# Four small loads moved to GpSimd's queue at the start, and two table copies moved behind the last key product

## The chip, the core and the metric

The kernel runs on one core of one Trainium2 chip. The metric is the device time in microseconds (us) of one launch, the median of several runs. The engines are named as in the profile: PE (TensorE matmul), PEld (its weight loads), DVE (VectorE), ACT (ScalarE), POOL (GpSimd), SP (SyncE, which only starts transfers). ACTq, SPq and POOLq are the issuing sides of these engines. Each engine runs its instructions strictly in the order in which they stand in its queue; an instruction that waits holds everything behind it.

## What is computed

Two transformer blocks on a sequence of 256 tokens of width 1024, all in fp32. The part that matters here is the beginning of the first block and three small inputs of the second:

```python
# first block
h    = rms_norm(x, norm_mix_pre)
proj = h @ w_in                              # q, k_c, v_c, k_s, v_s, k_w, v_w, gates, u, v
kc   = compress_tokens(k_c, cmp_pos_k, ...)  # 2-layer MLP over blocks of 32 keys
lg   = q @ k.T + rel_bias[bucket(distance)]  # three attention branches, softmax, gates
# second block
mod  = silu(c) @ ada_w + ada_b               # c: the conditioning vector, 1024 numbers
rel  = positions[key] - positions[query]     # 256 integers, bucketed
bias = rel_bias_2[bucket(rel)]               # table of 32 x 16
```

## The kernel before

Every large product takes its weights through `wload` (line 270, a transfer on SP's queue into one of six `raw` tiles) and `wsplit` (line 292): ACT writes the high part `hi` (line 301), DVE the low part `lo` (line 302), and PE adds three products per tile in `mm3` (lines 309 to 311). A `raw` tile is free for the next transfer when its `lo` has been written.

The first stage computes, in this order: the key and value projection (`kv`, 512 columns; its evaluation `ev_kv` makes `kd` tiles on DVE at line 788, which PE transposes at line 795), the bias table of the first block (`bias_tables`), the q projection (512 columns, `ev_q`, whose result DVE copies at line 784), `conditioning` (silu of the conditioning vector, in tile `c8`), `pos_prep` (positions split into parts by six DVE operations for the 256-wide tile `pr` and six for the 2-wide tile `pc`, the table `rel_bias_2` in tile `tb` split into three bf16 parts, and the clipped distances `relc`), the beginning of `compress` for the keys (tile `X`, line 846), and the last key product: the window projection of 280 columns (`ev_w`). Then a weave of attention, compression, conditioning rows (`adas_pe`) and the u and v projections follows, until about 150 us.

`bias_tables` stores an 8 x 384 row to DRAM (line 912), loads it back as the table `B1` of 1 MB spread over the partitions (line 914, ACT's queue), and at lines 916 and 917 DVE copies two strided pieces of `B1` into `Bc`, which the first attention logits need.

The order of instructions in each queue is made when the program is built: a scheduler places them by priority and by its own estimate of times, inside `queued(...)` blocks that keep instructions of ACT, DVE and SP behind marked ones. So a moved line of code can move instructions of other lines on the same engine. ACT's queue issues the transfers of `c8`, of the constants `tri` (128 x 818 numbers), of `pr`, `pc` and of the four 32-row pieces of `tb`. POOL sets constants, makes the identity matrix (masks.py), issues the transfers of `mod_quarters` (line 541), and computes the powers at line 226.

Of the kernel before, what the change touches and what calls it, by code (L numbers as in the profile page):

```python
# [20 lines left out]
P = 128  # L21
S = 256
# [66 lines left out]
def body(tc, I, O):  # L89
    nc = tc.nc  # L90
    v, s, g, pe, sy = nc.vector, nc.scalar, nc.gpsimd, nc.tensor, nc.sync
# [3 lines left out]
    def nm(x):  # L95
        cnt[0] += 1
        return f"{x}_{cnt[0]}"

    def pool(name, bufs=1, space=None, side=None):
        kw = {"reuse_waits": "tile"}  # L100
        if space is not None:
            kw["space"] = space
            if space is DRAM:
                kw = {"space": space}
        if side:
            kw["side"] = side
        return tc.tile_pool(name=name, bufs=bufs, **kw)
# [7 lines left out]
    def T(pl, shape, dt=F32, tag=None, bufs=1):  # L115
        n = nm(tag or "t")
        return pl.tile(list(shape), dt, name=n, tag=tag or n, bufs=bufs)
# [16 lines left out]
    def atb():  # L134
        return T(ps, [P, 512], tag="at", bufs=2)

    def scr(n=1024):
        return T(per, [P, 1024], tag="scr", bufs=NSCR)[:, :n]
# [4 lines left out]
    def run(gen):  # L143
        for _ in gen:
            pass
# [63 lines left out]
    tri = T(cst, [P, 2 * S + 2 * P + 50])  # L209
    cum = tri[:, 0:2 * S].rearrange("p (a l) -> p a l", a=2)  # L210
    o = 2 * S
# [58 lines left out]
    def wload(src3, shape, extra=(), tag="raw", bufs=None, pl=None):  # L270
        raw = T(pl or wp, [P, CH], tag=tag, bufs=bufs or NRAW)[:, :int(np.prod(shape))]
        raw = raw.rearrange("p (a n) -> p a n", a=shape[0])
        if src3 is not None:
            sy.dma_start(raw, src3)
        for d0, d1, src in extra:
            sy.dma_start(raw[:, :, d0:d1], src)
        return raw
# [27 lines left out]
    def ktile(W, k0, kn, c0, n):  # L305
        return W[k0 * P:(k0 + kn) * P, c0:c0 + n].rearrange("(a p) n -> p a n", p=P)

    def mm3(out, xh, xl, wh, wl, start, stop):
        pe.matmul(out, xh, wh, start=start, stop=False)  # L309
        pe.matmul(out, xh, wl, start=False, stop=False)  # L310
        pe.matmul(out, xl, wh, start=False, stop=stop)  # L311

    def groups(n, sizes):
        out, i = [], 0
        while i < n:
            k = sizes[min(len(out), len(sizes) - 1)]
            out.append(list(range(i, min(n, i + k))))
            i += k
        return out

    def proj(W, c0, n, KT, xT, evac, extra=None, sizes=(2,), bank=ma, pre=None):

        pc = max(1, CH // n)
        while KT % pc:
            pc -= 1
        xh, xl = xT
        accs = [bank()[:, :n], bank()[:, :n]]
        nch = KT // pc
        for grp in groups(nch, sizes):
            ws = {}  # L330
            for ci in grp:
                if pre and ci in pre:
                    raw = pre[ci]
                elif extra is None:
                    raw = wload(ktile(W, ci * pc, pc, c0, n), (pc, n))
                else:
                    raw = wload(None, (pc, n), [(d0, d0 + m, ktile(W, ci * pc, pc, cc, m)) for d0, cc, m in extra])
                ws[ci] = wsplit(raw, (pc, n))
            for t in range(2):
                sl = slice(t * P, (t + 1) * P)  # L340
                for ci in grp:
                    hi, lo = ws[ci]
                    for k in range(pc):
                        kk = ci * pc + k
                        mm3(accs[t], xh[:, kk, sl], xl[:, kk, sl], hi[:, k], lo[:, k], kk == 0, kk == KT - 1)
                if grp[-1] == nch - 1:
                    evac(t, accs[t])
                yield
# [167 lines left out]
    c8 = T(cst, [P, 8])  # L516
# [7 lines left out]
    T(cst, [P, 24])  # L524

    def conditioning():
        s.dma_start(tri, I["c_tri"])
        s.dma_start(c8, I["c_2"].rearrange("o (a p) -> p (o a)", p=P))
        s.activation(th8, c8, AF.Tanh, scale=0.5)
        v.scalar_tensor_tensor(th8, th8, 1.0, c8, op0=OP.add, op1=OP.mult)  # L530
        v.tensor_scalar(c8, th8, 0.5, None, op0=OP.mult)

    mods = T(dr, [6, D])

    gains = {1: "pre_norm_mix_2", 2: "post_norm_mix_2", 4: "pre_norm_ffn_2", 5: "post_norm_ffn_2"}
# [141 lines left out]
    pos = I["positions_2"]  # L677

    def pos_parts(dst_hi, dst_lo, dst_md, src):
        n = src.shape[-1]  # L680
        ti = T(pp, [P, S], I32, tag="pi", bufs=2)[:, :n]
        v.tensor_single_scalar(ti, src, 12, op=OP.arith_shift_right)
        v.tensor_copy(dst_hi, ti)
        ti = T(pp, [P, S], I32, tag="pi", bufs=2)[:, :n]
        v.tensor_single_scalar(ti, src, 4095, op=OP.bitwise_and)
        v.tensor_copy(dst_lo, ti)
        t2 = T(pp, [P, S], I32, tag="pi", bufs=2)[:, :n]
        v.tensor_single_scalar(t2, ti, 6, op=OP.arith_shift_right)
        v.tensor_copy(dst_md, t2)

    pmat = T(per, [P, 3, S])
    pcol = T(per, [P, 3, 2])
    rel_dr = T(dr, [S, S], BF)

    def pos_prep():
        pr = T(pp, [P, S], I32, tag="pi", bufs=2)
        s.dma_start(pr, bass.AP(tensor=pos.tensor, offset=pos.offset, ap=[[0, P], [1, S]]))
        pos_parts(pmat[:, 0], pmat[:, 1], pmat[:, 2], pr)
        pc = T(pp, [P, 2], I32)
        s.dma_start(pc, pos.rearrange("o (a p) -> p (o a)", p=P))  # L700
        pos_parts(pcol[:, 0], pcol[:, 1], pcol[:, 2], pc)

        tb = T(pp, [P, 4, 16])
        g.memset(tb, 0.0)
        for i in range(4):
            s.dma_start(tb[i * 32:(i + 1) * 32, i, :], I["rel_bias_2"])
        tbf = tb.rearrange("p a h -> p (a h)")
        v.tensor_scalar(tp[:, 0], tbf, -1.0, None, op0=OP.mult)
        rem = T(pp, [P, 64])
        v.scalar_tensor_tensor(rem, tbf, -1.0, tp[:, 0], op0=OP.mult, op1=OP.subtract)  # L710
        v.tensor_copy(tp[:, 1], rem)
        v.tensor_tensor(tp[:, 2], rem, tp[:, 1], op=OP.subtract)
        relc = scr(256).bitcast(BF).rearrange("p (k q) -> p k q", k=2)
        for k in range(2):
            ab = scr(512)
            a, b_ = ab[:, :S], ab[:, S:]
            v.tensor_scalar(a, pmat[:, 0], pcol[:, 0, k:k + 1], -4096.0, op0=OP.subtract, op1=OP.mult)
            v.tensor_scalar(b_, pmat[:, 1], pcol[:, 1, k:k + 1], -1.0, op0=OP.subtract, op1=OP.mult)
            v.tensor_tensor(a, a, b_, op=OP.add)
            v.tensor_scalar(relc[:, k], a, 120.0, -120.0, op0=OP.min, op1=OP.max)  # L720
        s.dma_start(rel_dr[:, :].rearrange("(k p) q -> p k q", p=P), relc)

    bias_dr = T(dr, [2, P, 16, S])

    def key_bias():
# [21 lines left out]
        for n in range(8):  # L747
# [7 lines left out]
            for t in range(2):  # L755
# [8 lines left out]
                    s.dma_start(bias_dr[t, :, :, k * P:(k + 1) * P], dst[t])  # L764
                yield

    with pool("a1") as ap:
        awg = pool("a1w")
        aw = awg.__enter__()
# [128 lines left out]
        B1 = T(ap, [P, 8, S])  # L898
        Bc = T(ap, [P, 2, 8, 16])

        def bias_tables():
            hf = scr()
            hot, fx = hf[:33, :384], hf[:8, 384:768]
            s.dma_start(hot, I["c_hot"])
            tab = T(aw, [33, 8], tag="tab")
            v.memset(tab[32:33, :], 1.0)
            s.dma_start(tab[0:32, :], I["rel_bias"])
            b = atb()
            pe.matmul(b[:8, :384], tab, hot, start=True, stop=True)
            v.tensor_copy(fx, b[:8, :384])  # L910
            scratch = T(dr, [8, 384])
            s.dma_start(scratch, fx)
            sc = scratch[:, :]
            s.dma_start(B1, bass.AP(tensor=sc.tensor, offset=sc.offset, ap=[[1, P], [384, 8], [1, S]]))
            g.memset(Bc, BIG)
            v.tensor_copy(Bc[:, 0, :, 0:7], B1[:, :, 96::-16])
            v.tensor_copy(Bc[:, 1, :, 0:15], B1[:, :, 224::-16])

        def attention():
            PTc = T(aw, [P, S], tag="PTc", bufs=1)  # L920
# [143 lines left out]
        with queued():  # L1064
            next(kv)
            run(kv)
            bias_tables()
            run(proj(W, 0, 512, 8, xT, ev_q))
            marks = mark()
            conditioning()  # L1070
            pos_prep()
            ck = compress(0, I["cmp_pos_k"][0], I["cmp_w1_k"][0], I["cmp_w2_k"][0])
            cv = compress(1, I["cmp_pos_v"][0], I["cmp_w1_v"][0], I["cmp_w2_v"][0])
            next(ck)
            ahead(3)
            run(proj(W, 1024, 280, 8, xT, ev_w))
        wa, wf = SCHED["a1"]
        with queued(marks=marks):
            weave((seq(ck, cv, mix(attention(), adas_pe((1, 0), aw, cws, ahead))), wa * 1.7),
# [159 lines left out]
    ap = latg.__enter__()  # L1239
# [143 lines left out]
    ap = atg.__enter__()  # L1383
# [205 lines left out]
```

## Time and profile before

| | us |
|---|---|
| median of 3 runs | 969.82 (967.96 to 969.91) |
| the profiled execution, its own time | 972.12 |
| its span, first to last instruction | 970.3 |
| PE busy | 921.8 (95% of the span) |
| DVE busy | 717.2 (74%) |
| ACT busy | 507.5 (52%) |
| POOL busy | 38.6 (4%) |
| granted PE clock, mean | 0.984 of full speed |

The profiled execution is 2.3 us longer than the median, and 1.8 us of it lie outside the span. The kernel is bound by PE nearly everywhere; what a change of small operations is worth has to be read from the few places where PE waits.

### The profile page before, as it was taken

Reading aid. Unit: us, or ns where it says so; the run is one execution under the profiler, and the core shown is the slowest. Engines: PE = TensorE matmul, PEld = TensorE weight load, DVE = VectorE, ACT = ScalarE, POOL = GpSimd, SP = SyncE. Lnnn points to the kernel's source line nnn. Section 1 sums busy time; section 2 is a strip of 40 time slices with the busy share of each in tenths; the row PEclk is TensorE's granted clock in tenths of the full one; section 3 lists DMA queues with packets and bytes.
Section 4 is the critical chain, followed back from the end, with each engine's and each line's share of the span. In section 5 each row is a group of like instructions: output and inputs, shape, how many; then the busy total and the mean of one; then the engine's idle time right before and its main releaser. Section 6 shows DMA issues by size and latency. Waiting matters only on the chain.

```text
span 970.3 us, 16176 instructions
## 1 busy us (share of the span) xinstructions
PE 921.8 (95%) x6161; PEld 778.1 (80%) x6161; DVE 717.2 (74%) x1305; ACT 507.5 (52%) x873; POOL 38.6 (4%) x63
## 2 busy tenths in 40 slices
PE   7899999979997999999799999999999999999997
PEld 6666667869996877897688679988977879999885
DVE  5767849487884559579988877889988885776544
ACT  5436536434542446466457548856763653444432
POOL 1000001000000002100000000000001010000000
PEclk9999999999999999999999999999999999999999
DMA  9887538678886596465444579687778667776651
GB/s 289 256 292 227 192 111 278 199 217 263 222 243 193 178 319 173 130 188 157 136 135 152 167 230 257 178 188 184 205 209 302 225 204 250 246 224 202 206 174 43
DMA packets 157113, 200.00 MB, mean 206 GB/s; under 512 B 14867, under 2 KB 118316, under 8 KB 157036
## 3 DMA queue, kind: packets, MB, share of 16 engines
q1 hardware_dynamic: 137840, 184.61, 63.4%
q10 hardware_dynamic: 16268, 8.30, 3.1%
q0 software_dynamic: 2928, 6.07, 2.1%
q8 instruction: 48, 0.79, 0.3%
q14 instruction: 29, 0.24, 0.1%
HBM read 193.39 MB, written 5.54 MB: 205 GB/s over the span
## 4 chain that ended last, share of the span: by engine, by line
PE 73%; DVE 9%; DMA 8%; issue 4%; ACT 3%; POOL 1%; SPq 0%; ACTq 0%; DVEq 0%; POOLq 0%
PE ma L311 6%; PE ma L309 6%; PE ma L310 6%; PE ma L388 6%; PE ma L390 6%; PE ma L389 5%; PE mb L388 5%; PE mb L389 5%; PE mb L390 5%; PE mb L310 4%; PE mb L309 4%; PE mb L311 4%; DMA t<-kb 3%; DVE lo L302 2%; DMA araw<-in_ada_w_dram 2%
## 5 line engine op out<-in xcount | busy, mean ns | idle before, releaser
L302 DVE TENSOR_TENSOR lo<-raw,hi 128x1024 fp32r<-128x1024 f32 (+2 forms) x242 | 291.7, 1212 | 117.1 <-ACT hi L301 113.3
L301 ACT CAST hi<-raw 128x1024 fp32r<-128x1024 f32 (+2 forms) x242 | 250.8, 1043 | 222.6 <-PE mb L311 75.8
L390 PE MATMUL ma<-xTh,lo 128*128 128x256 f32 x512 | 144.5, 282 | 6.8 <-DVE lo L302 6.7
L388 PE MATMUL ma<-xTh,hi 128*128 128x256 f32 x512 | 145.5, 284 | 1.6 <-ACT hi L301 1.6
L389 PE MATMUL ma<-xTl,hi 128*128 128x256 f32 x512 | 143.6, 280 | 0.0
L388 PE MATMUL mb<-xTh,hi 128*128 128x256 f32 x384 | 107.1, 279 | 0.0
L390 PE MATMUL mb<-xTh,lo 128*128 128x256 f32 x384 | 106.5, 277 | 0.0
L389 PE MATMUL mb<-xTl,hi 128*128 128x256 f32 x384 | 106.4, 277 | 0.0
L390 PEld LDWEIGHTS ma<-xTh,lo 128*128 128x128 f32 x512 | 97.5, 191 | 8.7 <-DVE lo L302 7.6
L388 PEld LDWEIGHTS ma<-xTh,hi 128*128 128x128 f32 x512 | 97.5, 190 | 4.7 <-ACT hi L301 2.0
L389 PEld LDWEIGHTS ma<-xTl,hi 128*128 128x128 f32 x512 | 97.6, 191 | 1.1 <-issue 0.8
L310 PE MATMUL ma<-lo,xTh 128*128 128x512 f32 (+2 forms) x192 | 74.8, 391 | 1.9 <-DVE lo L302 1.9
L309 PE MATMUL ma<-hi,xTh 128*128 128x512 f32 (+2 forms) x192 | 75.4, 395 | 0.0
L311 PE MATMUL ma<-hi,xTl 128*128 128x512 f32 (+2 forms) x192 | 75.1, 392 | 0.0
L388 PEld LDWEIGHTS mb<-xTh,hi 128*128 128x128 f32 x384 | 72.2, 188 | 1.2 <-issue 1.2
L390 PEld LDWEIGHTS mb<-xTh,lo 128*128 128x128 f32 x384 | 72.2, 188 | 0.4 <-DVE cva L1209 0.4
L389 PEld LDWEIGHTS mb<-xTl,hi 128*128 128x128 f32 x384 | 72.1, 188 | 0.2 <-issue 0.2
L310 PEld LDWEIGHTS ma<-lo,xTh 128*128 128x128 f32 x192 | 36.4, 189 | 10.2 <-DVE lo L302 2.9
L311 PEld LDWEIGHTS ma<-hi,xTl 128*128 128x128 f32 x192 | 36.4, 190 | 9.1 <-issue 2.4
L309 PEld LDWEIGHTS ma<-hi,xTh 128*128 128x128 f32 x192 | 36.6, 191 | 8.6 <-issue 1.9
L309 PE MATMUL mb<-hi,hTh 128*128 128x512 f32 x80 | 32.2, 402 | 0.0
L310 PE MATMUL ma<-lo,hTh 128*128 128x512 f32 x80 | 31.4, 392 | 0.5 <-DVE lo L302 0.5
(474 smaller groups left out, 1877.5 us busy)
## 6 DMA issues: line engine op xcount, KB each, us to landing
raw<-in_w_in_dram SPq DMA_DIRECT2D x80, 512.0 KB, 5.8
raw<-in_w_gate_up_dram SPq DMA_DIRECT2D x44, 512.0 KB, 7.7
raw<-in_w_ffn_in_dram SPq DMA_DIRECT2D x44, 512.0 KB, 4.8
raw<-in_w_down_dram SPq DMA_DIRECT2D x22, 512.0 KB, 4.6
raw<-in_w_ffn_out_dram SPq DMA_DIRECT2D x22, 512.0 KB, 4.5
cw<-in_ada_w_dram SPq DMA_DIRECT2D x16, 512.0 KB, 4.1
raw<-in_w_out_dram SPq DMA_DIRECT2D x16, 512.0 KB, 5.8
araw<-in_ada_w_dram SPq DMA_DIRECT2D x16, 512.0 KB, 11.7
```

Of the source, the lines that this page charges most:

```text
L301: s.copy(hi, raw)
L302: v.tensor_tensor(lo, raw, hi.bitcast(F32), op=OP.subtract)
L309: pe.matmul(out, xh, wh, start=start, stop=False)
L310: pe.matmul(out, xh, wl, start=False, stop=False)
L311: pe.matmul(out, xl, wh, start=False, stop=stop)
L388: pe.matmul(out, hi[:, k % pc, fs], xh[:, k], start=k == 0, stop=False)
L389: pe.matmul(out, hi[:, k % pc, fs], xl[:, k], start=False, stop=False)
L390: pe.matmul(out, lo[:, k % pc, fs], xh[:, k], start=False, stop=k == KT - 1)
```

## The change

`conditioning` no longer issues its two transfers. They, the two loads of the positions and the four of the table go out on POOL's queue (`g.dma_start` for `s.dma_start`). `pos_prep` becomes a generator in two pieces: the loads stand ahead of the first stage, the arithmetic where the whole stood before. The two copies into `Bc` move from `bias_tables` to a place behind the window projection.

```diff
     def conditioning():
-        s.dma_start(tri, I["c_tri"])
-        s.dma_start(c8, I["c_2"].rearrange("o (a p) -> p (o a)", p=P))
         s.activation(th8, c8, AF.Tanh, scale=0.5)
...
+    g.dma_start(c8, I["c_2"].rearrange("o (a p) -> p (o a)", p=P))
+    g.dma_start(tri, I["c_tri"])
     mods = T(dr, [6, D])
...
     def pos_prep():
         pr = T(pp, [P, S], I32, tag="pi", bufs=2)
-        s.dma_start(pr, bass.AP(tensor=pos.tensor, offset=pos.offset, ap=[[0, P], [1, S]]))
-        pos_parts(pmat[:, 0], pmat[:, 1], pmat[:, 2], pr)
+        g.dma_start(pr, bass.AP(tensor=pos.tensor, offset=pos.offset, ap=[[0, P], [1, S]]))
         pc = T(pp, [P, 2], I32)
-        s.dma_start(pc, pos.rearrange("o (a p) -> p (o a)", p=P))
-        pos_parts(pcol[:, 0], pcol[:, 1], pcol[:, 2], pc)
+        g.dma_start(pc, pos.rearrange("o (a p) -> p (o a)", p=P))
         tb = T(pp, [P, 4, 16])
         g.memset(tb, 0.0)
         for i in range(4):
-            s.dma_start(tb[i * 32:(i + 1) * 32, i, :], I["rel_bias_2"])
+            g.dma_start(tb[i * 32:(i + 1) * 32, i, :], I["rel_bias_2"])
+        yield
+        pos_parts(pmat[:, 0], pmat[:, 1], pmat[:, 2], pr)
+        pos_parts(pcol[:, 0], pcol[:, 1], pcol[:, 2], pc)
...
+        yield
...
+    pos_terms = pos_prep()
+    next(pos_terms)
     with pool("a1") as ap:
...
             g.memset(Bc, BIG)
-            v.tensor_copy(Bc[:, 0, :, 0:7], B1[:, :, 96::-16])
-            v.tensor_copy(Bc[:, 1, :, 0:15], B1[:, :, 224::-16])
...
             conditioning()
-            pos_prep()
+            next(pos_terms)
...
             run(proj(W, 1024, 280, 8, xT, ev_w))
+            v.tensor_copy(Bc[:, 0, :, 0:7], B1[:, :, 96::-16])
+            v.tensor_copy(Bc[:, 1, :, 0:15], B1[:, :, 224::-16])
```

On POOL, from the first constants to the first transfers of `mod_quarters`, before (`t_74` is the identity, `t_133` is `Bc`, `t_444` is `tb`):

```order
L219 MEMSET t_82 128x32
L817 MEMSET t_127 128x64
L915 MEMSET t_133 128x256
masks.py:199 ISA
masks.py:199 AFFINE_SELECT t_74<-t_74 128x128
L704 MEMSET t_444 128x64
L840 MEMSET X_473 128x512
L541 DMA t_775<-in_ada_b_dram 128x1x256
```

and now (`t_86` is `c8`, `t_79` is `tri`, `pi_118` is `pr`, `t_120` is `pc`, `t_122` is `tb`):

```order
L219 MEMSET t_82 128x32
L531 DMA t_86<-in_c_dram 128x8x1
masks.py:199 ISA
masks.py:199 AFFINE_SELECT t_74<-t_74 128x128
L532 DMA t_79<-in_c_tri_dram 128x818
L697 DMA pi_118<-in_positions_dram 128x256
L699 DMA t_120<-in_positions_dram 128x2x1
L702 MEMSET t_122 128x64
L821 MEMSET t_139 128x64
L919 MEMSET t_145 128x256
L704 DMA t_122<-in_rel_bias_dram 32x16 x4
L844 MEMSET X_471 128x512
```

One new transfer stands ahead of the identity matrix, and seven ahead of the tile `X` and of `mod_quarters`.

On DVE, from the end of the first block's x tiles to the `lo` of the fifth weight tile, before:

```order
L906 MEMSET tab_315 1x8
L302 TENSOR_TENSOR lo_204<-raw_99,hi_203 128x1024
L302 TENSOR_TENSOR lo_222<-raw_219,hi_221 128x1024
L302 TENSOR_TENSOR lo_228<-raw_225,hi_227 128x1024
L246 SCALAR_TENSOR_TENSOR sm_250<-sm_244,sm_247 128x1
L666 TENSOR_SCALAR r_64_243<-r_64_243 128x1 x4
L667 SCALAR_TENSOR_TENSOR r_64_243<-r_64_243 128x1
L302 TENSOR_TENSOR lo_332<-raw_329,hi_331 128x1024
```

and now, its beginning:

```order
L910 MEMSET tab_327 1x8
L682 TENSOR_SCALAR pi_430<-pi_118 128x256
L709 TENSOR_SCALAR t_109<-t_122 128x64
L302 TENSOR_TENSOR lo_216<-raw_101,hi_215 128x1024
L302 TENSOR_TENSOR lo_234<-raw_231,hi_233 128x1024
L302 TENSOR_TENSOR lo_240<-raw_237,hi_239 128x1024
L683 CAST t_114<-pi_430 128x256
L711 SCALAR_TENSOR_TENSOR t_449<-t_122,t_109 128x64
L685 TENSOR_SCALAR pi_433<-pi_118 128x256
```

The first operations on `pr` and on `tb` now stand ahead of the second `lo`, and the other fourteen of the positions and the table stand between the fourth and the fifth `lo`.

On DVE, at the end of the q projection, where lines 916 and 917 stood ahead of the first 280-column `lo` (`lo_494`), it is now (`t_145` is `Bc`, `t_135` the q tile of line 784 before):

```order
L302 TENSOR_TENSOR lo_492<-raw_489,hi_491 128x560
L302 TENSOR_TENSOR lo_498<-raw_495,hi_497 128x560
L1079 COPY t_145<-t_144 128x8x7
L1080 COPY t_145<-t_144 128x8x15
L788 COPY t_135<-tr_401 128x4x128
L302 TENSOR_TENSOR lo_528<-raw_525,hi_527 128x560
```

Two of the four `lo` tiles of the window projection now stand ahead of the copies, two behind.

On SP, the fourth weight tile of the key compression (`cw_592`), before:

```order
L274 DMA raw_801<-in_w_in_dram 128x2x512
L274 DMA raw_807<-in_w_in_dram 128x2x512
L274 DMA cw_592<-in_cmp_w_k_dram 128x4x256
L274 DMA raw_956<-in_w_in_dram 128x2x512
L274 DMA raw_962<-in_w_in_dram 128x2x512
```

and now:

```order
L274 DMA raw_801<-in_w_in_dram 128x2x512
L274 DMA raw_807<-in_w_in_dram 128x2x512
L274 DMA raw_956<-in_w_in_dram 128x2x512
L274 DMA raw_962<-in_w_in_dram 128x2x512
L274 DMA raw_1126<-in_w_in_dram 128x2x512
L274 DMA cw_592<-in_cmp_w_k_dram 128x4x256
```

It stands behind three more tiles of the u and v projections. In the PE queue the window projection's products, before interleaved with the first compression products (line 854), now all stand ahead of them, and eight 512-column products of the u projection stand ahead of the last four of the key compression. From about 150 us on, all queues read as before.

## Rows read from the trace of the kernel before

**Rows 1.** Page, part 1: busy time, share of the span, instructions of each engine
```profile
PE 921.8 (95%) x6161; PEld 778.1 (80%) x6161; DVE 717.2 (74%) x1305; ACT 507.5 (52%) x873; POOL 38.6 (4%) x63
```

**Rows 2.** Windows: stretch, us; busy PE, PEld, DVE, ACT, POOL (instructions); clock, DMA, GB/s
```profile
16.00:38.00 22.00, 22.00 (x102) 17.14 (x101) 14.08 (x40) 12.43 (x25) 2.03 (x2) 1.00 1.02 334
54.00:110.00 56.00, 55.65 (x362) 36.25 (x361) 42.02 (x158) 27.48 (x76) 1.50 (x3) 1.00 0.76 255
```

**Rows 3.** PE in order of time, 38 to 54: start, us, instruction [idle before <-releaser]
```profile
40.37 0.40 PE L310 MATMUL ma<-lo,xTh 128*128 128x280 f32 x1 [1.92 <-DVE lo L302]
...
46.37 1.02 PE L854 MATMUL at<-cw,X 128*32 128x256 f32 x10 [1.27 <-issue]
...
53.01 0.64 PE L854 MATMUL at<-cw,X 128*32 128x256 f32 x8 [0.37 <-DMA cw<-in_cmp_w_k_dram]
```

**Rows 4.** DVE in order of time, 36 to 48 us
```profile
38.68 0.21 DVE L916 COPY t<-t 128x56 f32<-128x56 f32 x1 [2.12 <-DMA t<-t]
...
44.49 2.05 DVE L846 TENSOR_TENSOR X<-t,posT 64x120 f32<-64x120 f32 x7
```

**Rows 5.** The chain that ended last, 30 to 60 us: start, us, what
```profile
47.06 5.91 DMA cw<-in_cmp_w_k_dram
```

**Rows 6.** DVE in order of time, 14 to 24 us
```profile
15.16 3.77 DVE L302 TENSOR_TENSOR lo<-raw,hi 128x1024 fp32r<-128x1024 f32 x3 [0.15 <-ACT hi L301]
...
21.41 1.23 DVE L302 TENSOR_TENSOR lo<-raw,hi 128x1024 fp32r<-128x1024 f32 x1 [1.02 <-ACT hi L301]
22.56 1.26 DVE L788 TENSOR_SCALAR kd<-ma,r 128x256 f32<-128x256 f32 x3
```

**Rows 7.** DVE, 32 to 42 us: one 256-wide, one 2-wide operation on the positions
```profile
32.82 0.30 DVE L683 CAST t<-pi 128x256 f32<-128x256 int32 x1
...
36.06 0.16 DVE L686 CAST t<-pi 128x2 f32<-128x2 int32 x1
```

**Rows 8.** PE in order of time, 11 to 24 us
```profile
11.72 1.08 PE L655 MATMUL tr<-t,t 128*128 128x128 f32 x4 [2.35 <-DMA t<-in_x_dram]
...
17.00 0.39 PE L310 MATMUL ma<-lo,xTh 128*128 128x512 f32 x1
...
23.42 0.38 PE L795 MATMUL tr<-t,kd 128*128 128x128 f32 x2
```

**Rows 9.** POOL in order of time, 0 to 30 us
```profile
2.21 0.88 POOL L541 DMA_DIRECT2D t<-in_ada_b_dram  x1
...
19.40 0.56 POOL L226 TENSOR_TENSOR r<-sm,t 128x1 f32<-128x1 f32 x1 [14.96 <-DVE sm L246]
23.97 1.47 POOL L226 TENSOR_TENSOR r<-sm,t 128x1 f32<-128x1 f32 x1 [4.01 <-DVE sm L246]
```

**Rows 10.** DMA issues, 0 to 40 us: engine, count, KB each, median us to landing
```profile
t<-in_c_tri_dram ACTq DMA_DIRECT2D x1, 409.0 KB, 6.3
t<-in_ada_b_dram POOLq DMA_DIRECT2D x2, 128.0 KB, 9.7
```

**Rows 11.** POOL's smallest transfers: min/median/max ns of an issue, then us to landing
```profile
L546 POOL DMA_DIRECT2D t<-t x2: 592/612/631, 106.2 to 140.9; - x2
...
DMA to landing us min/median/max: 1.7/4.6/6.4
```

**Rows 12.** ACT and its queue in order of time, 27 to 33 us
```profile
27.67 0.30 ACTq L912 DMA_DIRECT2D t<-scr  x1
...
30.90 0.21 ACT L529 ACTIVATE t<-t 128x8 f32<-128x8 f32 x1 [2.47 <-DMA t<-in_c_dram]
...
32.60 0.44 ACTq L914 DMA_DIRECT2D t<-t  x1
```

**Rows 13.** Windows around the two falls of the clock, columns as in Rows 2
```profile
12.00:16.00 4.00, 4.00 (x14) 3.29 (x13) 2.89 (x5) 2.31 (x3) 0.00 (x0) 0.61 1.04 333
...
116.00:126.00 10.00, 9.21 (x35) 6.63 (x37) 7.91 (x31) 4.45 (x16) 1.72 (x3) 0.66 0.37 111
```

**Rows 14.** PE in order of time, 112 to 118 us
```profile
116.80 0.63 PE L262 MATMUL tr<-t,scr 128*128 128x128 f32 x4 [0.91 <-DVE ag L1024]
```

## The prediction

> **What bounds the kernel now.** I read the engines' busy time first: PE works 95% of the span, DVE 74%, and POOL 4% [rows 1]. So DVE operations and transfers cost something only where PE waits for them. The windows then show where that can be: from 16 to 38 us PE has no idle time at all, and from 54 to 110 us it is busy 55.65 of 56 us [rows 2]. The changed code reaches between these windows and ahead of the first, so I read PE, DVE, POOL and ACT there one instruction at a time. From 38 to 54 us PE stands still three times [rows 3]:
>
> - 1.92 us at 40.37, for the `lo` of a window tile. That `lo` stands on DVE behind line 916, which itself waits 2.12 us for the table `B1`, landed at 38.68 [rows 4].
> - 1.27 us at 46.37, for the first tiles `X`, which DVE finishes last at 44.49 + 2.05 = 46.54 [rows 4].
> - 0.37 us at 53.01, for the fourth weight tile of the key compression, issued at 47.06 and landed 5.91 us later [rows 3, 5].
>
> Together 3.56 us. What PE gains ahead of 54 us it keeps, because it is full behind that until 110 us. Of the rest, one place is touched: around 116 to 126 us the granted clock is at its lower level for most of the time [rows 13], after PE waited 0.91 us [rows 14], and the order of PE's instructions up to 150 us changes.
>
> **The two copies (lines 916 and 917).** They move on DVE from ahead of the first window `lo` to behind the second. A window tile feeds twelve PE products (two steps, two halves of the tokens, three products), so PE has 24 to do before it needs the third `lo`; even at half of the 0.22 us that a PE instruction took from 16 to 38 us (22.0 / 102 [rows 2]) that is 2.6 us from 38.45, and B1's landing at 38.68 is hidden. The 1.92 us go. The copies are not needed before the attention, past the window projection.
>
> **The order on PE.** All window products now stand ahead of the compression products (line 854), so PE reaches `X` later than DVE finishes it: PE's work from 40.37 to 53.01 is 53.01 − 0.37 − 40.37 − 1.27 = 11.0 us, and most of it (over 7 us) now stands ahead of the first line 854. Counted from 38.45 that is past 46, and with the delay worked out below past 47, against 46.54. The 1.27 us go.
>
> **The arithmetic on positions and table.** It leaves the stretch from 32 to 44 us, in which DVE waits for B1 anyway, so its going is worth nothing there by itself. It comes into the stretch before 24 us. There are six 256-wide operations of 0.30 us, six 2-wide of 0.16 us [rows 7], and four on the 64-wide table between these, 0.2 us each: 1.8 + 0.96 + 0.8 = 3.6 us, less some overlap at their ends, 3.4 us. Two of them (0.30 + 0.20) stand ahead of the second `lo`, the others between the fourth and the fifth. DVE has had three `lo` done at 15.16 + 3.77 = 18.93 and sat idle 1.02 us ahead of the next at 21.41 [rows 6], so the 3.4 us are partly covered. Step by step: 0.5 us ahead of the `lo` make it 19.4; 1.3 us of the later ones plus the square-root steps (about 0.5) 21.2; 1.6 us more 22.8; the `lo` of 1.23 us 24.0; the first `kd` (1.26 / 3 = 0.42) 24.45, against 22.98 before. PE's line 795, which transposes it, started at 23.42 [rows 8], with 0.4 us to spare: PE waits about **1.0 us**, between 0 (if the `lo` waits for its `hi` anyway) and 1.5.
>
> **The loads on POOL.** DVE's first table operation waits for the four pieces of the table, the last of eight transfers on POOL, and everything on DVE stands behind it. PE needs the second `lo` at 17.00 [rows 8]; it takes 1.23 us [rows 6] and the table operation 0.2 us, so the transfers may land up to T = 17.00 − 1.23 − 0.2 = 15.57 for nothing. POOL issued its first transfer at 2.21, in 0.88 us [rows 9], and its smallest take 0.61 us [rows 11]. Four by 0.88 and four by 0.61 are 5.9 us, so the last issue ends near 8.1. The landing is not in the trace. Bounds: 1.7 us, the least of its small ones [rows 11], gives T = 9.8; 6.3 us, as `tri` took on ACT's queue [rows 10], 14.4; 9.7 us, as the first `mod_quarters` took on POOL's [rows 10], 17.8. The two nearest rows, the last two, have the mean 16.1: a wait of **0.5 us**, with 0 and 2.2 as ends. The Trainium skill ("DMA: Bandwidth & Descriptors", section "Anatomy of one DMA — SWDGE (gpsimd) path") gives about 2.0 us fixed plus bytes by 436 GB/s for a transfer of this kind, by which, as an estimate, T were about 10 and the wait nothing; the 9.7 us that 128 KB took here do not agree with it, and the row decides.
>
> POOL also makes the identity matrix, now behind the issue of `c8`, so some 0.9 us later. PE's first x tiles need it and wait for x anyway (2.35 us even at 11.72 [rows 8]): 0, and 0.9 if that cover is gone. The transfers of `mod_quarters` leave later, those of `c8`, `tri` and `pr` earlier, in the stretch in which the second half of x lands: 538 KB against 384 KB moved away. I take 0 for that, and 1 us to either side.
>
> **ACT's queue.** It gives up eight issues, all in its idle time, and no longer waits 2.47 us for `c8` [rows 12]: 0 by itself. It did keep the load of B1 back: the store of line 912 left at 27.67, the load at 32.60 [rows 12]. Now the load follows when the store has landed, but the store itself is later by the 1.5 us above. I keep B1's landing at 38.7.
>
> **The fourth compression tile.** It stands on SP behind three more weight tiles, the last of which needs a `raw` buffer that a `lo` behind `X` sets free: 46.54 + 0.42 (`kd`) + 1.23 (`lo`) = 48.2. With 5.91 us to landing it is there at 54.1. PE's work ahead of it has grown by thirteen instructions; at the 0.22 us from above they take 2.9, and five of them are narrower: 2.6 us. PE arrives at 38.45 + 1.5 + 11.0 + 2.6 = 53.55, and waits **0.55 us** (0 to 2.5).
>
> **The sum.** −1.92 − 1.27 − 0.37 + 1.0 + 0.5 + 0.55 = −1.5 us. On the profiled execution, 972.12, that makes 970.6; the median lies 2.3 us under it, so **968.3 us**.
>
> **Rivals.**
>
> *The table lands late (slower).* If POOL's issues are stretched as its one-column product was beside a busy DVE, 1.47 against 0.56 us [rows 9], a factor of 2.6, eight issues take 15.3 us and end at 17.5; with the median landing of 4.6 us [rows 11] T is 22.1 and the wait 6.5 us. Between this and the 2.2 us above lies 4.4 us, 3.9 more than I took. PE's clock was at 0.61 from 12 to 16 us, behind such waits [rows 13], 4 × 0.39 = 1.6 us lost; another such fall makes the sum −1.5 + 3.9 + 1.6 = +4.0, or 973.8. It decides from a wait of 2.0 us, T = 17.6. For it speaks the 9.7 us; against it that DVE has little to do before 8 us, while PE still waits for x. The Trainium skill ("SBUF — State Buffer", section "Summary: rules for kernel authors") speaks against this change too: making a transfer on GpSimd's queue is held up while DVE runs in some of its fast modes, and ACT's or SP's queue is to be used instead; no run here shows that yet, and by the rule the time would be this rival's.
>
> *The whole gain (faster).* B1's load, free of the wait for `c8`, lands up to 2 us earlier, DVE's 2.12 us of idle time go, `X` is ready at 44.5 and the fourth compression tile lands at 52, ahead of PE. With the table landed by 15.57 as well: −3.56 + 1.0 = −2.6, or 967.2.
>
> *The fall of the clock goes (faster).* At 116 to 126 us the clock of 0.66 loses 10 × 0.34 = 3.4 us [rows 13]. If PE, in its new order, no longer waits there, −1.5 − 3.4 = −4.9, or 964.9. The wait hangs on DVE and the attention, not on what is moved; I give it little.
>
> **How the numbers follow.** A measurement of this kernel can tell about 0.2%, 1.9 us, from no change. Forecast: 0.48, with a spread of about 1.5 us from the bounds, so 0.14 faster, 0.28 same, 0.06 slower. The late table: 0.20. The whole gain: 0.18, faster. The clock: 0.14, faster. That makes faster 0.46, same 0.28, slower 0.26. The range from 964.0 to 974.0 takes in the clock's case and the late table's up to its middle, and leaves out what lies behind that and below.
>
> **What would show it.** DVE's first table operation (line 709 of the changed kernel) should wait until some 16 us; a start past 17.6 means the late table. PE should wait about 1.0 us ahead of its first line 795, not at the first window `lo` nor at the first line 854, and again some 0.5 us at the last four products of the key compression. The clock from 116 to 126 us should be near 0.66. I am wrong if the second `lo` is late by over 2 us, if x lands later than 11.7, if the moved copies keep the attention waiting, or if the clock falls in a new place.

## The result: 0.9% slower, outside the range

The changed kernel takes 979.58 us (median of four runs, 976.09 to 982.54) against 969.87 for the kernel before (four runs, 967.96 to 971.29). The two medians lie 9.7 us apart. The ratio on record, by which this text goes, is 1.0089, with a 95% interval from 1.0066 to 1.0112, so some 8.6 us slower. The forecast was 968.3 us, in a range from 964.0 to 974.0. The profiled execution is the longest of the four, 982.54 us with a span of 980.8; it stands 10.4 us over the profiled execution of before, and its rows have to be read with that in mind.

The page, part 1, of the kernel after (for [rows 1]): PE works 7 us longer for the same 6161 products, and the span is 10.5 us longer, so some 3.5 us more of it are idle.

```profile
PE 928.9 (95%) x6161; PEld 781.3 (80%) x6161; DVE 717.5 (73%) x1305; ACT 508.2 (52%) x873; POOL 43.5 (4%) x71
```

Windows of the kernel after, for [rows 2, 13] (stretch, its length, busy us and instructions of PE, PEld, DVE, ACT, POOL, then granted clock, DMA share, GB/s):

```profile
12.00:16.00 4.00, 4.00 (x14) 3.34 (x15) 2.76 (x7) 2.27 (x4) 0.00 (x0) 0.61 1.09 258
16.00:38.00 22.00, 19.60 (x87) 14.79 (x86) 15.25 (x44) 11.49 (x23) 2.12 (x2) 1.00 0.96 302
54.00:84.00 30.00, 25.92 (x158) 17.71 (x158) 15.38 (x39) 8.30 (x14) 0.53 (x1) 0.94 0.75 234
84.00:104.00 20.00, 18.64 (x65) 11.44 (x63) 11.78 (x61) 9.37 (x31) 0.00 (x0) 0.66 0.43 154
116.00:126.00 10.00, 9.73 (x80) 6.32 (x79) 8.12 (x34) 6.20 (x21) 1.17 (x2) 1.00 0.50 174
```

The 22 us from 16 to 38, which PE filled before, have 2.4 us of idle time; from 54 to 84 it is 4.1 us. The low clock has left 116 to 126 us and stands now at 84 to 104, where before the clock was at 1.00: by estimate 18.64 × 0.34 = 6.3 us lost, against 9.21 × 0.34 = 3.1 before.

PE in order of time, the four waits of over a microsecond from 16 to 200 us (for [rows 3, 8]; start, us, instruction, in brackets the idle time before it and what ended it):

```profile
26.39 0.44 PE L799 MATMUL tr<-t,kd 128*128 128x128 f32 x2 [1.75 <-DVE kd L792]
...
49.88 0.44 PE L799 MATMUL tr<-t,kd 128*128 128x128 f32 x2 [2.11 <-DVE kd L792]
...
61.80 0.64 PE L858 MATMUL at<-cw,X 128*32 128x256 f32 x8 [3.65 <-DMA cw<-in_cmp_w_k_dram]
...
85.75 0.47 PE L309 MATMUL ma<-hi,xTh 128*128 128x512 f32 x1 [1.36 <-DVE d L940]
```

The first and the third I had named, at 1.0 and 0.55 us. The second and the fourth I had not. The waits for the first window tile and for `X` are gone, as forecast. All of the loss arises ahead of 152 us: the products of line 561 that wait 0.93 us for `mTl` start at 139.45 before and at 152.06 now, 12.6 us later, of which some 2 us come back by the end.

DVE of the kernel after in order of time (for [rows 4, 6]):

```profile
15.50 0.19 DVE L709 TENSOR_SCALAR t<-t 128x64 bf16<-128x64 f32 x1
...
20.56 1.22 DVE L302 TENSOR_TENSOR lo<-raw,hi 128x1024 fp32r<-128x1024 f32 x1 [2.60 <-ACT hi L301]
...
41.69 0.21 DVE L1079 COPY t<-t 128x56 f32<-128x56 f32 x1 [4.84 <-DMA t<-t]
...
47.28 2.04 DVE L850 TENSOR_TENSOR X<-t,posT 64x120 f32<-64x120 f32 x7
```

The table was there in time: line 709 did not wait. The third `lo` did, 2.60 us, for a `hi`, and ACT waited with that for the weight tile:

```profile
19.48 1.05 ACT L301 CAST hi<-raw 128x1024 fp32r<-128x1024 f32 x1 [2.87 <-DMA raw<-in_w_in_dram]
```

`B1` landed at 41.69, 3 us later than before.

The chain that ended last, 50 to 64 us, in the kernel after (start, us, what; for [rows 5]):

```profile
52.49 0.60 PE at L858 x7
53.08 0.02 issue
53.10 8.66 DMA cw<-in_cmp_w_k_dram
61.76 0.04 issue
61.80 0.64 PE at L858 x8
```

What starts the load of the fourth tile is PE itself, with the compression products on the first.

### The profile page after: what moved, and what is told of

Its sections match the earlier page's. It is cut to its first block, busy times and chain, and to the rows that moved or that the text cites. A ratio compares the mean times of both kernels' runs of the same rounds, so it can differ in the third digit from the quotient of the medians.

```text
span 980.8 us, 16189 instructions
## 1 busy us (share of the span) xinstructions
PE 928.9 (95%) x6161; PEld 781.3 (80%) x6161; DVE 717.5 (73%) x1305; ACT 508.2 (52%) x873; POOL 43.5 (4%) x71
## 4 chain that ended last, share of the span: by engine, by line
PE 70%; DMA 12%; DVE 9%; ACT 4%; issue 3%; POOL 1%; SPq 0%; ACTq 0%; DVEq 0%; POOLq 0%
PE ma L388 5%; PE ma L390 5%; PE ma L389 5%; PE ma L310 5%; PE ma L311 5%; PE ma L309 5%; PE mb L388 5%; PE mb L389 5%; PE mb L390 4%; PE mb L309 4%; PE mb L310 4%; PE mb L311 4%; DMA raw<-in_w_in_dram 3%; DMA t<-kb 3%; DVE lo L302 2%
## 5 line engine op out<-in xcount | busy, mean ns | idle before, releaser
L311 PE MATMUL mb<-hi,hTl 128*128 128x512 f32 x80 | 31.7, 396 | 0.0
```

## The experiments

Each result is the ratio to runs of the kernel before on the same chip, with its 95% interval; 0.1% is about 1 us.

### What was wrong with the fourth tile, and what it is worth

The three `cw` buffers hold the first three weight tiles. The fourth waits until PE has used the first. In the next two kernels it takes one of the six `raw` buffers instead.

```diff
+                    if i == 3:
+                        cws.append(wload(cwt[i], (4, 256)))
+                        continue
                     cws.append(wload(cwt[i], (4, 256) if i < 8 else (1, 1024), tag="cw", bufs=3, pl=aw))
...
-            ahead(3)
+            ahead(4)
```

**Run e3**: what was expected.

> The changed kernel, but the fourth weight tile of the key compression takes one of the six raw buffers, so that its load no longer waits until PE has used the first tile. Theory A (the loss comes from this tile's load being tied to PE's first compression products, and from the falls of the clock behind that wait): the wait of 3.65 us at 61.8 goes, the clock no longer falls at 63 to 66, about 5 us less than 979.6: 974 to 975, and near 970 if the fall at 87 to 101 goes too. Theory B (the loss comes from the late start: the loads on POOL and the arithmetic make the table B1 and X late, and the tile only follows): the wait comes back under another name ahead of the next products, time 978 to 980.

Measured: 1.0080 (1.0064 to 1.0097). The wait for this tile is gone, and so is the 1.36 us behind the softmax, but the time stayed (1.0089 for the changed kernel). PE of this run waits at the next place that its faster way brings it to, a tile of the value compression, and the clock falls there; the window of 20 us behind it shows this, in an execution that was the slowest of five (986.93 us, median 979.24):

```profile
72.04 0.64 PE L861 MATMUL at<-cw,X 128*32 128x256 f32 x8 [1.79 <-DMA cw<-in_cmp_w_v_dram]
```

```profile
72.00:92.00 20.00, 19.96 (x79) 13.37 (x80) 7.80 (x35) 5.76 (x14) 0.00 (x0) 0.57 0.55 192
```

So theory A, that the loss comes from this one load, fell. Theory B was right in its time, and a wait came back under another name; whether its reason, the late start, holds is for the runs below.

**Run e4**: what was expected.

> The kernel before with the same own buffer for the fourth tile. Both theories: only the 0.37 us wait at 53.0 can go; 969 to 970, and any loss shows what the lent raw buffer costs.

Measured: 0.9985 (0.9964 to 1.0007). Within this interval the lent buffer costs the kernel before nothing.

### Taking the change apart

The first of these is the changed kernel with the arithmetic held back (`with queued(): next(pos_terms)`). The second is the kernel before with only `c8` and `tri` loaded by POOL. The third is the changed kernel with the copies back in their old lines.

**Run e5**: what was expected.

> The changed kernel, with the arithmetic on positions and table held behind the last q tile, so that DVE's queue up to 33 us is that of the kernel before; loads stay early on POOL. PE's order is that of the changed kernel. Theory A: the 1.75 us wait for kd at 26.4 goes, the wait for the fourth tile stays at 3 us or more, the clock falls stay: 977 to 978. Theory B: B1, X and the tile are all earlier, the wait shrinks under 1 us: 970 to 973.

Measured: 1.0062 (1.0035 to 1.0089). PE still waited 1.68 us for `kd` at 26.2, though no arithmetic stood on DVE ahead of it: ACT waited 2.72 us for the third weight tile. So the late `kd` was not the arithmetic's doing, and both theories were wrong in that. The wait for the fourth tile was 2.62 us, and the time is near what theory A gave.

**Run e6**: what was expected.

> The kernel before with only c8 and tri loaded by POOL at the start; positions and table as before on ACT's queue with their arithmetic, copies in the old place in the code. PE's order comes out as in the changed kernel (window products ahead of the compression). Theory A: the wait for the fourth tile is there, 3 us or more, 975 to 978. Theory B: no late start, so 969 to 971.

Measured: 1.0031 (1.0007 to 1.0054), between both expectations. Up to 28 us PE is idle for 5.2 us, against 6.0 in the kernel before; the wait for the fourth tile is 3.73 us and the clock falls behind it and again from 84 us. The profiled execution is the slowest of ten (980.96 us, median 974.90). With neither positions nor table moved, PE's order, and its waits from 40 us on, are nearly those of the changed kernel. One of them is this, though `B1` landed at 38.85 here, as before:

```profile
47.03 0.44 PE L795 MATMUL tr<-t,kd 128*128 128x128 f32 x2 [1.75 <-DVE kd L788]
```

**Run e2**: what was expected.

> The changed kernel with the two copies of the bias table back in their old place in the code. DVE's queue comes out the same as in the changed kernel, copies behind the second window tile, so moving them in the code is worth nothing once the loads are moved: 977 to 982, with the waits of the changed kernel (tile about 3.6 us, 1.4 us behind the compressed softmax, a fall of the clock behind each). A time under 975 would say that the copies' place matters.

Measured: 1.0090 (1.0062 to 1.0118), the same as the changed kernel. Moving the two copies in the code was worth nothing: once the loads leave ACT's queue, the scheduler puts the copies behind the second window tile from the old line too. As it has the same queues, this run is also a second look at the changed kernel. PE's waits differ: the fourth tile's is 2.31 us in place of 3.65, the one of 2.11 us for `kd` is 0.32, and the window that stood at 0.66 reads:

```profile
84.00:104.00 20.00, 18.89 (x116) 12.25 (x117) 14.26 (x68) 11.24 (x35) 0.00 (x0) 0.91 0.56 196
```

The wait ahead of it was 1.36 us in both. How long the clock stays low behind a wait thus differs between executions of one program; a term for it can't be read from one profile.

The next three restore the early place of the first half of the compression on PE, or move as little as possible:

```diff
-            run(proj(W, 1024, 280, 8, xT, ev_w))
+            w = proj(W, 1024, 280, 8, xT, ev_w)
+            next(w)
+            next(w)
+            next(ck)
+            run(w)
```

**Run e8** (with it, on the changed kernel): what was expected.

> The changed kernel, with the first half of the key compression called in the middle of the window projection, so that PE's queue has these products where they stood before, and the third and later u products no longer stand ahead of the compression's end. Theory C (two parts that add: the early position and table loads cost about 3 us at the start, PE's new order costs the rest, by the wait for the tile and the fall of the clock at 87 to 101): the tile's wait is under 0.5 us, no fall at 72 to 112, time 0.3 to 0.5% over before: 973 to 976. Theory D (any PE wait of a microsecond makes such a fall, and the changed start makes one anyway): falls come back at another place, 978 to 980.

Measured: 1.0139 (1.0088 to 1.0189).

**Run e10** (with it, on e6): what was expected.

> As the run with c8 and tri alone on POOL, and the same call of the first half of the key compression in the middle of the window projection. Theory C: neither part is left, 968 to 971. Theory D: 974 to 976.

Measured: 1.0090 (1.0062 to 1.0119).

**Run e11** (without it, `c8` alone moved): what was expected.

> The kernel before with only c8 loaded by POOL at the start. ACT no longer waits for it ahead of the load of B1. PE's order stays near that of before. The wait of 1.92 us for the first window tile should shrink if c8's wait held B1's load back: 968 to 970; if B1 lands as late as before, 969.5 to 971.5.

Measured: 1.0064 (1.0041 to 1.0087).

All three were misses. Theory C, that putting this one place back restores the time, fell. The call in the middle brings PE to `X` before it is ready (1.98 and 1.45 us of waiting), and a wait of 2.77 us at 132 and 121 us that no other kernel here has. With `c8` alone, a transfer of 4 KB, the wait for the first window tile stays (2.01 us), and PE's order changes enough for waits of 2.32 us for the fourth tile, of 1.35 us at 117 and 1.26 us at 142 us. That the whole order up to 150 us counts, and not one pair of neighbours, fits these runs; none of them isolates it.

### The two causes, each alone

The first kernel has the queues of PE, DVE, ACT and SP of the kernel before, and POOL's eight early transfers of the changed one:

```diff
+    g.dma_start(c8, I["c_2"].rearrange("o (a p) -> p (o a)", p=P))
+    g.dma_start(tri, I["c_tri"])
+    early = T(per, [P, 1024], tag="row", bufs=2)
+    g.dma_start(early[:, 0:S].bitcast(I32), bass.AP(tensor=pos.tensor, offset=pos.offset, ap=[[0, P], [1, S]]))
+    g.dma_start(early[:, S:S + 2].bitcast(I32), pos.rearrange("o (a p) -> p (o a)", p=P))
+    for i in range(4):
+        g.dma_start(early[i * 32:(i + 1) * 32, 512 + i * 16:528 + i * 16], I["rel_bias_2"])
```

**Run e12**: what was expected.

> The kernel before, with the same eight transfers issued by POOL at the start as in the changed kernel, but as a second copy: c8 and tri are loaded early and again at their old place, positions and table go early into a free row and are not used from there. PE, DVE, ACT and SP have the queues of the kernel before. So this is the traffic and POOL's delay at the start, and nothing else. Theory E (two causes: the start loses about 3 us to the early transfers; the new order loses the rest): 0.2 to 0.4% over before, with PE's waits ahead of 28 us 2 to 3 us longer. Rival F (the order alone): within 0.1% of before.

Measured: 1.0036 (1.0022 to 1.0051), 3.5 us, as theory E expected. PE in order of time shows where, with not one instruction more on it:

```profile
20.25 0.50 PE L309 MATMUL ma<-hi,xTh 128*128 128x512 f32 x1 [0.46 <-ACT hi L301]
...
21.51 0.50 PE L310 MATMUL ma<-lo,xTh 128*128 128x512 f32 x1 [0.76 <-DVE lo L302]
...
25.85 0.44 PE L802 MATMUL tr<-t,kd 128*128 128x128 f32 x2 [1.53 <-DVE kd L795]
...
43.65 0.60 PE L310 MATMUL ma<-lo,xTh 128*128 128x280 f32 x1 [2.70 <-DVE lo L302]
```

The waits ahead of 28 us are like the changed kernel's (0.66 and 1.75 us there). DVE's third `lo` starts at 20.23 here, behind a late `hi`, as it does there at 20.56. The last line is a wait of 1.92 us before [rows 3]; behind it the granted clock stands at 0.50 from 44 to 50 us. The changed kernel has no such wait, so this part of e12's loss is not its own.

Which of the transfers make the third weight tile late, the traces tell in part. `c8` and `tri`, 413 of the 550 KB, do not: in e6, which loads them early, PE waits for no `lo` and no `kd` from 12 to 28 us. What differs is when POOL's old transfers, the 384 KB of `mod_quarters`, go out. POOL of the changed kernel:

```profile
7.94 0.73 POOL L541 DMA_DIRECT2D t<-in_ada_b_dram  x1 [0.33 <-DMA t<-in_c_dram]
10.25 0.70 POOL L541 DMA_DIRECT2D t<-in_pre_norm_mix_dram  x1 [1.58 <-DMA t<-in_c_tri_dram]
11.22 0.68 POOL L541 DMA_DIRECT2D t<-in_ada_b_dram  x1 [0.28 <-DMA pi<-in_positions_dram]
```

Before, they left from 2.21 to 3.76, in e6 from 4.28 to 5.70. Here they stand behind eight others, and the trace puts the rest of the delay down to waits for the first three of these to land. So they move when the third weight tile is under way. The DMA queues from 12 to 20 us (packets, MB, share of the 16 engines' time; by their bytes q1 carries SP's transfers and q0 POOL's), before, in e6 and in e12:

```profile
q1 hardware_dynamic: 1814, 2.84, 103.5%
q0 software_dynamic: 33, 0.02, 1.4%
```

```profile
q1 hardware_dynamic: 1517, 2.58, 99.1%
q0 software_dynamic: 122, 0.10, 6.1%
```

```profile
q1 hardware_dynamic: 910, 1.74, 86.8%
q0 software_dynamic: 415, 0.37, 20.7%
```

Beside POOL's 0.37 MB, SP's queue moved 1.1 MB less than before. No kernel moves `mod_quarters` alone, so this step is read from the traces and not tested.

The second loads nothing early. It moves two transfers of `B1` from ACT's queue to POOL's, after which the scheduler gives PE the changed kernel's order:

```diff
-            s.dma_start(scratch, fx)
+            g.dma_start(scratch, fx)
...
-            s.dma_start(B1, bass.AP(tensor=sc.tensor, offset=sc.offset, ap=[[1, P], [384, 8], [1, S]]))
+            g.dma_start(B1, bass.AP(tensor=sc.tensor, offset=sc.offset, ap=[[1, P], [384, 8], [1, S]]))
```

**Run e14**: what was expected.

> The kernel before with only the store and the load of the bias table B1 (lines 912 and 914) moved from ACT's queue to POOL's; nothing is loaded early. PE's order comes out as in the changed kernel, window products ahead of the compression, and the copies fall behind the second window tile on DVE. Theory E: the wait for the fourth tile (2.5 to 3.7 us), the 1.4 us behind the compressed softmax and falls of the clock behind them: 0.3 to 0.5% over before, 973 to 976. A rival that puts all on the early transfers: at or below before.

Measured: 1.0064 (1.0038 to 1.0090), 6.2 us, a little above what theory E expected. Its waits are those of the changed kernel from 47 us on, though not of the same length: 2.10 us for `kd` at 47.9, 1.30 us for the fourth tile, and 1.36 us behind the compressed softmax at 81.3. The two parts make 0.36 + 0.64 = 1.00%, where the whole change measured 0.89% (0.66 to 1.12). This fits, but the split is rough. From 42 us on, PE, DVE and SP have the same queues in e14, in e6 and in the changed kernel, and e6 measured 1.0031 (1.0007 to 1.0054) with two of the early loads besides. And e14 is not the order alone to the letter: its `B1` goes out on POOL's queue and lands at 39.70, 1 us later than before. So the order costs some 3 to 6 us.

### The waits, filled with idle products

**Run f1**: what was expected.

> The changed kernel with fourteen idle 128-column products on PE ahead of the last four compression products, where PE waits 3.65 us for the fourth tile. If the fall of the clock at 61 to 67 comes from that wait, it is gone there: 1.7 us less, 977 to 979, the later falls unchanged. If it does not come from it, the clock falls there all the same and the time is 979 to 982.

Measured: 1.0082 (1.0049 to 1.0114). The clock behaved as expected: with PE at work on idle products (28 instructions in the trace, 3.29 us) it stays up behind the tile in this execution; e16 below has no fall behind a wait of 2.48 us for the same tile either, so this alone does not show the cause. Windows of the changed kernel, then of this run:

```profile
60.00:64.00 4.00, 2.20 (x13) 1.51 (x14) 0.42 (x1) 0.00 (x0) 0.53 (x1) 0.87 0.74 232
64.00:68.00 4.00, 4.00 (x18) 3.38 (x18) 0.62 (x3) 1.48 (x3) 0.00 (x0) 0.71 0.95 356
```

```profile
60.00:64.00 4.00, 3.68 (x31) 3.40 (x29) 2.14 (x2) 0.00 (x0) 0.00 (x0) 1.00 0.97 281
64.00:68.00 4.00, 3.38 (x24) 2.56 (x24) 0.87 (x3) 0.48 (x2) 0.53 (x1) 1.00 0.93 310
```

The time did not follow: the order around the added products changed as well, and this run has a fall at 44 to 52 us, behind a wait of 3.27 us. So the next two were built so that the added products are the only difference in any queue. The first adds six to the kernel with the order alone, where PE waits 1.36 us; they write a part of the bank that is never read.

```diff
+                        if h == 0 and br == 1:
+                            with queued((mybir.EngineType.PE,)):
+                                for _ in range(6):
+                                    pe.matmul(lg[:, 3 * P:], ident, ident, start=True, stop=True)
```

**Run e16**: what was expected.

> The kernel of the run with the order alone, with six idle 128-column products on PE where it waits 1.36 us for DVE behind the compressed softmax (at 81 us); every other queue is unchanged. If the fall of the clock at 82 to 95 comes from that wait and makes up most of the order's 6.2 us, the clock stays at 1.0 there and the time falls by 4 to 6 us, to within 0.3% of before. If the order's loss lies in the waits ahead of 72 us, or the fall comes from the stretch behind the wait, the time stays 0.5 to 0.7% over before.

Measured: 1.0034 (1.0014 to 1.0055) against 1.0064 without them. The added products take 1.60 us where PE waited 1.36; what is won lies behind them. Windows of the kernel with the order alone, then of this one:

```profile
84.00:88.00 4.00, 4.00 (x11) 2.19 (x10) 2.39 (x11) 1.66 (x7) 0.00 (x0) 0.50 0.69 275
88.00:92.00 4.00, 4.00 (x10) 2.33 (x9) 1.75 (x9) 0.11 (x2) 0.00 (x0) 0.50 0.01 5
92.00:96.00 4.00, 4.00 (x20) 2.54 (x19) 0.81 (x5) 2.50 (x9) 0.00 (x0) 0.50 0.00 0
```

```profile
84.00:88.00 4.00, 4.00 (x19) 2.53 (x19) 3.23 (x17) 2.76 (x10) 0.00 (x0) 1.00 0.84 340
88.00:92.00 4.00, 4.00 (x27) 2.46 (x27) 2.79 (x17) 2.44 (x10) 0.00 (x0) 1.00 0.18 28
92.00:96.00 4.00, 4.00 (x31) 2.89 (x29) 3.93 (x16) 2.73 (x9) 0.00 (x0) 1.00 0.34 117
```

By the two ratios that is about 2.9 us of the order's 6.2, nearly a half, but their intervals overlap, so the times by themselves do not show it. The profiled executions do: the kernel with the filled wait reaches its fourth tile 1.1 us later than the other (60.06 against 58.98) and the next wait at line 561 4.5 us earlier (102.55 against 107.03). All five profiled kernels with this wait unfilled (the changed kernel, e2, e5, e6, e14) have the fall behind it. The wait itself is not won back, since the added products fill it.

The second adds two and four such products to the kernel before, at the waits of 0.50 and 0.91 us ahead of 117 us [rows 14].

**Run e18**: what was expected.

> The kernel before, with two and four idle 128-column products on PE where it waits 0.50 and 0.91 us at 114.8 and 116.8 us; every other queue is unchanged. If the fall of the clock at 118 to 124 comes from these two waits, it is gone and the time is 2 to 3.5 us less than before, 0.2 to 0.35%. If not, the same as before.

Measured: 0.9980 (0.9963 to 0.9996), 968.33 us against 970.63. The clock is at 1.00 from 116 to 128 us. By 0.2%, just clear of noise, it is faster than the kernel before, by doing more. The three profiled kernels with these two waits unfilled (before, e4, e12) all have the fall behind them.

## Why the prediction was wrong, step by step

**What bounds the kernel** was read rightly: the loss lies at PE's waits and in the falls of the clock behind them, ahead of 152 us.

**The two copies and the first window tile.** The wait of 1.92 us went, as forecast. The credit does not go to the copies, whose move changes no queue (e2), but to the loads: with them off ACT's queue the scheduler puts the copies behind the second window tile by itself.

**The order on PE: the step that failed.** That PE reaches `X` late enough was right, and the 1.27 us went. What failed is the premise that PE keeps what it gains ahead of 54 us, because it is full behind that until 110 us. It was full in the old order. In the new one PE is idle for 4.1 us from 54 to 84 us, and the clock falls twice from 54 to 104 us. The order was forecast at −3.0 us; where it stands without the early loads, it measured +6.2 us (e14), and +3.0 us with two of them (e6).

The wait for the fourth tile, within this, was mis-sized by a wrong releaser. I took the load of the fourth tile to wait for a `raw` buffer behind a `lo`, and got its issue at 48.2. It waits for the first `cw` buffer. It could be seen before: PE's first ten compression products started at 46.37, and the load left at 47.06 [rows 3, 5]; and the code gives these tiles three buffers, for four tiles. With the window products ahead of the compression, those first products come at 51.5 to 53, the load leaves at 53.10, and PE's work between them and the last four lasts only until 58.15. The wait is 3.65 us in place of 0.55; in runs e2, e5 and e6 it is 2.31, 2.62 and 3.73. To ask who frees the buffer was the step left out. It does not explain the loss by itself: without this wait the time stayed (e3).

**`B1`'s landing** I kept at 38.7. Its load left at 32.30, no earlier than before, since the store went late, and took 9.4 us in place of 6.1. PE did not feel it at the window, as forecast. Why it took 9.4 us was not tried. The 2.11 us for `kd` at 49.88, which my sum did not have, need no late `B1`: with `B1` on time PE waits 1.75 us there (e6). In the new order DVE makes this `kd` straight behind `X`, and PE, with the window products ahead of it done, comes to it while DVE is still at `X`.

**The arithmetic and the loads on POOL: the price right, the payer wrong.** I charged 1.0 us to the arithmetic ahead of `kd`, 0.5 us to the wait for the table, and nothing to the traffic. Measured were 1.75 us at `kd` and 0.66 us ahead of it, but neither from the arithmetic (e5) nor from the table, which landed in time. It is the traffic: the early transfers alone, with DVE's queue untouched, give like waits (e12), 3.5 us in all. The third weight tile comes late. This is the second step that failed: I put the traffic at nothing, with 1 us to either side, because I looked only at the second half of x, which landed in time for PE at 11.97 against 11.72 [rows 8]. I had the 384 KB of `mod_quarters` as moved away and did not ask what they would meet where they went. Of the small transfers, the four pieces of the table landed 6.4 us after their issue, close to the 6.3 us of `tri` on ACT's queue [rows 10]. POOL issued them in 0.50 us each, so the stretch of its issues that the late-table rival counted on did not come: DVE started its first operation only at 6.28, when POOL was at the last two of the eight. What POOL's queue cost, it cost through what it sent and, as the traces have it, through when `mod_quarters` left.

The Trainium skill ("SBUF — State Buffer", section "Summary: rules for kernel authors") says that the making of transfers on GpSimd's queue is held up while DVE runs in some of its fast modes. No run here shows such a hold-up.

**The clock.** I asked whether the fall at 116 to 126 us would go, and gave that 0.14. It went, with the order. I did not ask where the new order would make PE wait next: 1.36 us at 85.75, behind the compressed softmax, with a lower clock for longer than the old one. By the ratios that may be half of the order's loss (e14, e16).

**The size.** Of forecast −1.5 us and measured +8.6 us, 10 us apart, the runs give 3.5 us to the early traffic (forecast: 0.5 for the table and 1.0 for `kd`) and 6.2 us to the order (forecast: −3.0, the three old waits less 0.55). That makes 2.0 + 9.2 = 11.2 us, within the intervals; with e6's 3.0 us for the order it would be 8.0. How the order's loss divides between the softmax's wait, the tile, `kd` and the old waits that went, the runs do not tell: taking the tile's wait away gave nothing (e3).

## What to carry to other kernels

A load moved earlier is not free when it is small and its old queue was idle: ask what was landing in that stretch, which tile PE needs soonest after it, and which transfers of the new queue it pushes back, and into what. When a scheduler sets the order, the first thing a moved load moves is the order, so follow each weight tile on PE's new order back to the instruction that frees its buffer. Work that fills one stretch of PE in one order need not fill it in another. A wait of PE costs more than its length where the clock falls behind it; a few idle products in exactly that place took 0.2% (0.04 to 0.37) off the kernel before.

## What the runs showed of the hardware

Behind a PE wait of 1.36 us the granted clock stood at 0.50, the lower of its two levels (1.2 of 2.4 GHz), in each of five profiled executions: until 96 us and later in four of them, until 88.5 us in e2, which has the queues of the changed kernel. In the two kernels in which idle products on PE were the only change, the fall behind the filled wait did not come. Not every wait brings a fall: e16 waited 2.11 us at 49.30 and 2.48 us at 60.06, and its clock was 1.00 from 28 to 130 us.

Eight early transfers of together some 550 KB on POOL's queue, with its 384 KB of `mod_quarters` behind them in the stretch from 12 to 20 us, made the third weight tile late enough for DVE's `lo` to wait 2.29 us, and cost 3.5 us (e12). In that stretch SP's queue moved 1.74 MB beside POOL's 0.37 MB, and 2.84 MB before.
